# The second pair of gate and up tiles in products of 256 columns instead of 512

## The chip, the cores and the metric

The kernel runs on one core of a Trainium2 chip. The metric is the time of one execution in device microseconds (us). TensorE does the matrix products, VectorE (DVE) and ScalarE (ACT) the elementwise work, GpSimd (POOL) small work and some transfers, and SyncE (SP) issues most transfers. Products are written into PSUM, which has eight banks of 128 x 512 float32; everything else that the engines read lies in SBUF.

## The reference

One decoder layer on 512 tokens of 1024 features: a half-step SwiGLU network, a token mixer (sparse and dilated attention), and a second half-step SwiGLU network, each between two RMS norms.

```python
D_MODEL, SEQ, D_FF = 1024, 512, 2816

def swiglu(x, w_gate, w_up, w_down):
    return (jax.nn.silu(x @ w_gate) * (x @ w_up)) @ w_down

h = rms_norm(x, ffn1_pre)
x = x + 0.5 * rms_norm(swiglu(h, ffn1_w_gate, ffn1_w_up, ffn1_w_down), ffn1_post)
h = rms_norm(x, mix_pre)
x = x + rms_norm(token_mixer(h, ...), mix_post)
h = rms_norm(x, ffn2_pre)
x = x + 0.5 * rms_norm(swiglu(h, ffn2_w_gate, ffn2_w_up, ffn2_w_down), ffn2_post)
```

## The kernel before

"Part one" and "part two" are here the two SwiGLU networks; both run through `ffn`, part one with `opened` set (what `opening` has prepared), part two without. The token mixer lies between them.

**Products.** Every float32 operand is kept as a high and a low part (`split`, lines 139 to 141: ScalarE casts the high part at line 140, VectorE subtracts it from the source for the low part at line 141). `mm3` (lines 161 to 165) makes a product from three: high x high, high x low, low x high. Each of the three loads its own 128 x 128 weights and streams the activations `xhl` past them, up to 512 columns, one column a token.

**The hidden columns.** The 2816 hidden columns are 22 tiles of 128, taken as 11 pairs; index `p` is the pair, `f` the tile in it, `h` the half of the 1024 features (four blocks of 128), and `n` is gate or up. The first two pairs (`PLAIN = 2`) are computed directly; `mms` multiplies one half of one tile with all 512 tokens: four blocks, three products each, so 12 products of 512 columns. The other nine pairs use a scheme that multiplies sums of blocks (a fast matrix product with seven products in place of eight, named P1 to P7); `product` makes each from 24 products of 256 columns.

**Pair 0 and pair 1.** Pair 0 of part one is made in `opening`, which also makes the first half of pair 1's first tile; these are lines 1666 and 1696, 512 columns wide, and a full-precision product at line 1697 spreads the norm's row. In `ffn`, pair 1 of part one is then three calls' worth of weights, 72 products, and pair 1 of part two is four, 96. In part two pair 0 is made in 256 columns at a time, since its activations arrive token tile by token tile. `entered` splits one weight tile of 128 x 1024 into `whi` and `wlo` (three buffers each) and refills its raw buffer. `swiglu` multiplies and activates a finished pair of banks, `sums` makes sums of the results and stores them.

**The idle products.** Ahead of P1 of pair 2, `run` puts four products (`RESET`, lines 540 to 542) whose result is overwritten: 128 x 256, weights and activations both taken from the last weight tile of pair 1. They go into the bank that P1 opens.

**Order.** A scheduler orders each engine's instructions when the program is built, by its own estimate of times; what stands on an engine runs in that order. `PS_TAGS` gives the banks in turn (three S, two T, one V, two F).

Of the kernel before, what the change touches and what calls it, by code (L numbers as in the profile page):

```python
# [62 lines left out]
class Layer:  # L63
# [92 lines left out]
    def wsplit(self, src, shape):  # L156
        hi, lo = self.wpair(shape)
        self.split(hi, lo, src)
        return hi, lo

    def mm3(self, out, lhi, llo, rhi, rlo, start, stop, skip=False):
        mm = self.nc.tensor.matmul
# [175 lines left out]
    def ffn(self, gu, wd, td, post, finish, xsrc, aside=None, opened=None):  # L338
# [25 lines left out]
        def mms(w, h, n, b, lo=0, hi=S):  # L364
            c = slice(lo, hi)
            for j in range(4):
                k = 4 * h + j
                self.mm3(b[:, c], w[0][n][:, j], w[1][n][:, j], self.xh[k][:, c], self.xl[k][:, c], k == 0, k == KT - 1)

        def weight_sums(p):  # L370

            put = nc.gpsimd.dma_start
# [93 lines left out]
            return w  # L466

        for p in range(PLAIN):
            acts = []
            for f in range(2):  # L470
                key = 2 * p + f
                if p:
                    ws = [None if (key, 0) in banks and h == 0 else entered(p, h, f) for h in range(2)]
                    bs = [banks[key, n] if (key, n) in banks else self.bank() for n in range(2)]
                    for h in range(2):
                        for n in range(2):
                            if ws[h]:
                                mms(ws[h], h, n, bs[n])
                else:
                    bs = [banks[f, n] for n in range(2)]  # L480
                act = self.slot("W" if f else "ring")
                swiglu(act, bs[0], bs[1], slice(0, S))
                acts.append(act)
            sums(p, *acts)
            if p == 0 and not opened:
                tops = self.token_sums(t_tags)
            split_even(p)
# [43 lines left out]
        def run(p, name):  # L531
# [5 lines left out]
            if start:  # L537
                st[bank] = self.bank()
            with self.tc.issue_after(self.last_mm):
                if p == PLAIN and name == "P1":  # L540
                    for _ in range(RESET):
                        nc.tensor.matmul(st[bank][:, 0:256], self.last_w[:, 0], self.last_w[:, 2:4].rearrange("p k f -> p (k f)"), start=True, stop=True)
                product(w, top, st[bank], start)

        def finished(i, p, name):
# [1057 lines left out]
    def opening(self, gu, wd, td):  # L1603
# [37 lines left out]
        with self.tc.manual_schedule(engines={ET.Activation, ET.DVE, ET.PE}):  # L1641
# [51 lines left out]
            for n in range(2):  # L1693
                for k in range(4):
                    c = slice((4 * n + k) * P, (4 * n + k + 1) * P)
                    self.mm3(banks[4 + n], w[0][:, c], w[1][:, c], xh[k], xl[k], k == 0, False)
            nc.tensor.matmul(rowb, ones, diag, start=True, stop=True)
            row = self.slot("PT")
            nc.scalar.copy(row, rowb)
# [77 lines left out]
```

## Time and profile before

| | us |
|---|---|
| median of 3 runs | 1118.05 (1117.5 to 1119.21) |
| the profiled execution | 1118.12 |
| its span, first to last instruction | 1116.4 |

| engine | busy us | share of the span |
|---|---|---|
| TensorE products | 1095.6 | 98% |
| TensorE weight loads | 973.9 | 87% |
| VectorE | 883.4 | 79% |
| ScalarE | 642.4 | 58% |
| GpSimd | 187.7 | 17% |

Where things lie in the span: `opening` up to 34 us, pair 1 of part one from there to 51 us, the other nine pairs to 224 us, the down product behind them; part two has pair 0 from 783 us, pair 1 from 807 to 831 us and the nine pairs to 1003 us.

How to read the views: a row of the order of time gives the start, the duration, the engine, the line, the operation, the tile written and the tiles read, the shapes, and the count; in square brackets stands idle time of the engine before it and what ended it. A row of stretches gives, for each engine, its busy time in the stretch and in brackets how many instructions touch it, then the granted clock of TensorE, the busy share of the transfer engines and their GB/s. Products overlap, so their durations add up to more than the time between their starts.

### The profile page before, as it was taken

Reading aid. Unit: us, or ns where it says so; the run is one execution under the profiler, and the core shown is the slowest. Engines: PE = TensorE matmul, PEld = TensorE weight load, DVE = VectorE, ACT = ScalarE, POOL = GpSimd, SP = SyncE. Lnnn points to the kernel's source line nnn. Section 1 sums busy time; section 2 is a strip of 40 time slices with the busy share of each in tenths; the row PEclk is TensorE's granted clock in tenths of the full one; section 3 lists DMA queues with packets and bytes.
Section 4 is the critical chain, followed back from the end, with each engine's and each line's share of the span. In section 5 each row is a group of like instructions: output and inputs, shape, how many; then the busy total and the mean of one; then the engine's idle time right before and its main releaser. Section 6 shows DMA issues by size and latency. Waiting matters only on the chain.

```text
span 1116.4 us, 18585 instructions
## 1 busy us (share of the span) xinstructions
PE 1095.6 (98%) x6878; PEld 973.9 (87%) x6878; DVE 883.4 (79%) x1554; ACT 642.4 (58%) x1151; POOL 187.7 (17%) x264
## 2 busy tenths in 40 slices
PE   9999999999999999999999999999999999999997
PEld 7899999978889887777888898887989999998886
DVE  6989999988787889787554556876878999989575
ACT  7455555566565778675565625644435555557452
POOL 0444454310020055472000000000000000000001
PEclk9999999999999999999999999999999999999999
DMA  9999999999863499993224426383334444478862
GB/s 350 254 286 326 302 270 301 290 312 334 291 210 105 152 274 291 283 248 84 76 85 133 126 85 163 122 314 107 107 120 123 137 142 128 130 226 292 283 188 103
DMA packets 115595, 227.53 MB, mean 204 GB/s; under 512 B 21905, under 2 KB 51633, under 8 KB 115505
## 3 DMA queue, kind: packets, MB, share of 16 engines
q1 hardware_dynamic: 99136, 174.18, 47.8%
q0 software_dynamic: 16224, 51.91, 18.4%
q8 instruction: 54, 0.88, 0.3%
q14 instruction: 37, 0.30, 0.1%
q10 hardware_dynamic: 144, 0.26, 0.1%
HBM read 191.66 MB, written 57.72 MB: 223 GB/s over the span
## 4 chain that ended last, share of the span: by engine, by line
PE 76%; DVE 10%; ACT 4%; DMA 4%; issue 3%; POOL 1%; SPq 0%; POOLq 0%; DVEq 0%; ACTq 0%
PE pb_F L165 9%; PE pb_F L164 9%; PE pb_F L163 9%; PE pb_S L165 7%; PE pb_S L164 7%; PE pb_S L163 7%; PE pb_T L165 5%; PE pb_T L163 5%; PE pb_T L164 5%; PE pb_V L163 2%; PE pb_V L164 2%; PE pb_V L165 2%; DVE wlo L141 2%; DMA tdram<-in_d_dram 2%; PE pb_T L1666 1%
## 5 line engine op out<-in xcount | busy, mean ns | idle before, releaser
L141 DVE TENSOR_TENSOR wlo<-raw,whi 128x1024 fp32r<-128x1024 f32 (+1 forms) x211 | 248.5, 1183 | 125.3 <-ACT whi L140 122.6
L140 ACT CAST whi<-raw 128x1024 fp32r<-128x1024 f32 (+1 forms) x211 | 214.5, 1018 | 167.2 <-PE pb_F L164 41.9
L163 PE MATMUL pb_F<-xhl_t,whi 128*128 128x512 f32 (+1 forms) x440 | 155.1, 352 | 1.9 <-DVE Q_s L1409 1.0
L165 PE MATMUL pb_F<-xhl_t,wlo 128*128 128x512 f32 (+1 forms) x440 | 153.8, 350 | 1.3 <-DVE wlo L141 1.3
L164 PE MATMUL pb_F<-xhl_t,whi 128*128 128x512 f32 (+1 forms) x440 | 153.7, 349 | 0.0
L184 POOL TENSOR_TENSOR rs_t<-rs_t,mhalf_t 128x1 f32<-128x1 f32 x20 | 13.2, 659 | 558.2 <-DVE rs_t L180 558.2
L163 PEld LDWEIGHTS pb_F<-xhl_t,whi 128*128 128x128 f32 x440 | 82.8, 188 | 12.3 <-DVE Q_s L1409 1.2
L165 PEld LDWEIGHTS pb_F<-xhl_t,wlo 128*128 128x128 f32 x440 | 82.8, 188 | 11.8 <-DVE wlo L141 2.1
L164 PEld LDWEIGHTS pb_F<-xhl_t,whi 128*128 128x128 f32 x440 | 82.8, 188 | 9.6 <-issue 0.2
L163 PE MATMUL pb_S<-xhl_t,whi 128*128 128x256 f32 (+1 forms) x280 | 83.3, 297 | 0.0
L164 PE MATMUL pb_S<-xhl_t,whi 128*128 128x256 f32 (+1 forms) x280 | 83.1, 297 | 0.0
L165 PE MATMUL pb_S<-xhl_t,wlo 128*128 128x256 f32 (+1 forms) x280 | 82.8, 297 | 0.0
L1158 POOL TENSOR_SCALAR SP_s<-SP_s,st_t 128x384 f32<-128x384 f32 (+2 forms) x48 | 49.0, 1093 | 74.3 <-DMA raw<-in_w_in_dram 48.7
L163 PE MATMUL pb_T<-xhl_t,whi 128*128 128x256 f32 x200 | 55.4, 277 | 0.0
L164 PE MATMUL pb_T<-xhl_t,whi 128*128 128x256 f32 x200 | 55.4, 277 | 0.0
L165 PE MATMUL pb_T<-xhl_t,wlo 128*128 128x256 f32 x200 | 55.4, 277 | 0.0
L165 PEld LDWEIGHTS pb_S<-xhl_t,wlo 128*128 128x128 f32 x280 | 52.6, 188 | 2.2
L164 PEld LDWEIGHTS pb_S<-xhl_t,whi 128*128 128x128 f32 x280 | 52.6, 188 | 2.2
L163 PEld LDWEIGHTS pb_S<-xhl_t,whi 128*128 128x128 f32 x280 | 52.6, 188 | 2.2
L140 ACT CAST whi<-tmp_t 128x1024 fp32r<-128x1024 f32 x36 | 36.4, 1052 | 30.4 <-DVE tmp_t L512 23.5
L373 POOL DMA_DIRECT2D PT_s<-in_d_dram x44 | 39.1, 987 | 32.5 <-DMA PT_s<-in_d_dram 24.6
L141 DVE TENSOR_TENSOR PT_s<-pb_T,PT_s 128x512 fp32r<-128x512 f32 (+1 forms) x72 | 39.2, 558 | 6.8 <-ACT PT_s L140 6.1
(852 smaller groups left out, 3342.9 us busy)
## 6 DMA issues: line engine op xcount, KB each, us to landing
raw<-in_gu_dram SPq DMA_DIRECT2D x64, 512.0 KB, 4.6
raw<-tdram SPq DMA_DIRECT2D x40, 512.0 KB, 5.2
raw<-in_w_in_dram SPq DMA_DIRECT2D x18, 1024.0 KB, 5.4
PT_s<-in_d_dram POOLq DMA_DIRECT2D x66, 256.0 KB, 6.6
raw<-in_d_dram SPq DMA_DIRECT2D x30, 512.0 KB, 4.6
tdram<-in_d_dram POOLq DMA_DIRECT2D x18, 768.0 KB, 10.6
tdram<-PT_s POOLq DMA_DIRECT2D x44, 256.0 KB, 5.5
CP_s<-in_gu_dram SPq DMA_DIRECT2D x20, 512.0 KB, 3.9
```

The costliest lines, as they stand in the source:

```text
L140: self.last_cast = self.nc.scalar.copy(dsthi, src).ins
L141: self.last_sub = self.nc.vector.tensor_sub(dstlo, src, dsthi.bitcast(F32)).ins
L163: mm(out, lhi, rhi, start=start, stop=False, skip_group_check=skip)
L164: mm(out, lhi, rlo, start=False, stop=False, skip_group_check=skip)
L165: self.last_mm = mm(out, llo, rhi, start=False, stop=stop, skip_group_check=skip).ins
L184: nc.gpsimd.tensor_tensor(out=r, in0=v, in1=self.mhalf, op=OP.pow)
L373: add = lambda dst, src: put(dst, src, accum_op=OP.add)
L1158: self.last_pool = nc.gpsimd.tensor_scalar(pp, pp, st[:, 1, t:t + 1], None, op0=OP.mult).ins
L1666: nc.tensor.matmul(banks[b], l[:, c], r, start=k == 0 and i == 0, stop=k == KT - 1 and i == 2)
```

## The change

The products of pair 1 in `ffn` are made by a new function, `mms2`, which makes each product of 512 columns as two of 256; both write into the same bank, so only the first one of a bank starts it. The four idle products become a function, `reset`. In part one they stand ahead of pair 1's first product and no longer ahead of P1; in part two they stay where they were. To have a bank for them, part one takes the two banks of pair 1's second tile earlier.

```diff
+    def reset(self, b):
+        for _ in range(RESET):
+            self.nc.tensor.matmul(b[:, 0:256], self.last_w[:, 0], self.last_w[:, 2:4].rearrange("p k f -> p (k f)"), start=True, stop=True)
...
+        def mms2(w, h, n, b):
+            for j in range(4):
+                k = 4 * h + j
+                for m in range(2):
+                    c = slice(256 * m, 256 * m + 256)
+                    self.mm3(b[:, c], w[0][n][:, j], w[1][n][:, j], self.xh[k][:, c], self.xl[k][:, c], k == 0 and m == 0, k == KT - 1, True)
...
-            acts = []
+            acts, fresh = [], []
...
-                    bs = [banks[key, n] if (key, n) in banks else self.bank() for n in range(2)]
+                    bs = [banks[key, n] for n in range(2)] if (key, 0) in banks else fresh or [self.bank() for _ in range(2)]
                     for h in range(2):
                         for n in range(2):
                             if ws[h]:
-                                mms(ws[h], h, n, bs[n])
+                                if opened and f == 0 and n == 0:
+                                    fresh.extend(self.bank() for _ in range(2))
+                                    self.reset(fresh[0])
+                                mms2(ws[h], h, n, bs[n])
...
-                if p == PLAIN and name == "P1":
-                    for _ in range(RESET):
-                        nc.tensor.matmul(st[bank][:, 0:256], self.last_w[:, 0], self.last_w[:, 2:4].rearrange("p k f -> p (k f)"), start=True, stop=True)
+                if p == PLAIN and name == "P1" and not opened:
+                    self.reset(st[bank])
...
-                    self.mm3(banks[4 + n], w[0][:, c], w[1][:, c], xh[k], xl[k], k == 0, False)
+                    self.mm3(banks[4 + n], w[0][:, c], w[1][:, c], xh[k], xl[k], k == 0, False, True)
```

The rows that follow are the order of instructions as built; the kernel after has its lines 4 to 13 further down (163 is there the idle product, 167 to 169 are `mm3`, and 1710 is 1697).

TensorE at the end of part one's opening, before: the full-precision product, then the first products of pair 1.

```order
L165 MATMUL pb_S_139<-xhl_t_110,wlo_327 128x512
L1697 MATMUL pb_V_140<-W_s_363,cd_t_132 128x512 [waits DVE_49]
L163 MATMUL pb_F_138<-xhl_t_110,whi_454 128x512 [waits Activation_49]
L164 MATMUL pb_F_138<-xhl_t_110,whi_454 128x512
L165 MATMUL pb_F_138<-xhl_t_110,wlo_455 128x512
```

And the same place in the change:

```order
L169 MATMUL pb_S_139<-xhl_t_110,wlo_327 128x512
L1710 MATMUL pb_V_140<-W_s_363,cd_t_132 128x512 [waits DVE_49]
L163 MATMUL pb_S_459<-whi_454 128x256 [waits Activation_49]
L163 MATMUL pb_S_459<-whi_454 128x256 x3
L167 MATMUL pb_F_138<-xhl_t_110,whi_454 128x256
L168 MATMUL pb_F_138<-xhl_t_110,whi_454 128x256
L169 MATMUL pb_F_138<-xhl_t_110,wlo_455 128x256
```

The idle products now follow the full-precision one, read the high part of pair 1's first weight tile, and the products behind them are 256 wide.

TensorE in pair 1 of part two, before, at the point where the second weight tile is first used (its high part is `whi_8949`, its low part `wlo_8950`; 24 products of the pair stand ahead of these rows):

```order
L163 MATMUL pb_F_8954<-xhl_t_8433,whi_8949 128x512 [waits Activation_49]
L164 MATMUL pb_F_8954<-xhl_t_8433,whi_8949 128x512
L163 MATMUL pb_S_8955<-xhl_t_8433,whi_8949 128x512
L164 MATMUL pb_S_8955<-xhl_t_8433,whi_8949 128x512
L163 MATMUL pb_S_9017<-xhl_t_8433,whi_9007 128x512 [waits Activation_49]
L164 MATMUL pb_S_9017<-xhl_t_8433,whi_9007 128x512
L163 MATMUL pb_S_9018<-xhl_t_8433,whi_9007 128x512 [waits DVE_49]
L164 MATMUL pb_S_9018<-xhl_t_8433,whi_9007 128x512
L165 MATMUL pb_F_8954<-xhl_t_8433,wlo_8950 128x512 [waits DVE_49]
```

And in the change, where 48 products of the pair stand ahead:

```order
L167 MATMUL pb_F_9026<-xhl_t_8505,whi_9021 128x256 [waits Activation_49]
L168 MATMUL pb_F_9026<-xhl_t_8505,whi_9021 128x256
L167 MATMUL pb_S_9027<-xhl_t_8505,whi_9021 128x256
L168 MATMUL pb_S_9027<-xhl_t_8505,whi_9021 128x256
L167 MATMUL pb_S_9137<-xhl_t_8505,whi_9127 128x256 [waits Activation_49]
L168 MATMUL pb_S_9137<-xhl_t_8505,whi_9127 128x256
L167 MATMUL pb_S_9138<-xhl_t_8505,whi_9127 128x256 [waits DVE_49]
L168 MATMUL pb_S_9138<-xhl_t_8505,whi_9127 128x256
L169 MATMUL pb_F_9026<-xhl_t_8505,wlo_9022 128x256 [waits DVE_49]
```

In both programs the scheduler has lifted eight products that need only high parts over the one that waits for the low part; they were 512 wide and are 256 wide now.

VectorE in part one, around `sums` of pair 0 and the split of P1's weights (the row of `wlo`), before:

```order
L404 TENSOR_TENSOR W_s<-W_s,pb_S 128x512
L411 TENSOR_TENSOR of_s<-ring_s 128x256
L410 TENSOR_TENSOR of_s<-ring_s,W_s 128x256
L412 TENSOR_TENSOR ring_s<-of_s,ring_s 128x256
L413 TENSOR_TENSOR ring_s<-W_s,ring_s 128x256
L141 TENSOR_TENSOR wlo<-raw,whi 128x1024
L141 TENSOR_TENSOR Q_s<-ring_s,Q_s 128x512
L404 TENSOR_TENSOR ring_s<-ring_s,pb_S 128x512
L411 TENSOR_TENSOR of_s<-ring_s 128x256
```

And in the change (lines 413, 415 and 421 to 424 are 402, 404 and 410 to 413 of before):

```order
L415 TENSOR_TENSOR W_s<-W_s,pb_S 128x512
L422 TENSOR_TENSOR of_s<-ring_s 128x256
L421 TENSOR_TENSOR of_s<-ring_s,W_s 128x256
L413 TENSOR_TENSOR pb_F<-pb_F,PT_s 128x512
L423 TENSOR_TENSOR ring_s<-of_s,ring_s 128x256
L424 TENSOR_TENSOR ring_s<-W_s,ring_s 128x256
L141 TENSOR_TENSOR Q_s<-ring_s,Q_s 128x512
L415 TENSOR_TENSOR ring_s<-ring_s,pb_S 128x512
L422 TENSOR_TENSOR of_s<-ring_s 128x256
L141 TENSOR_TENSOR wlo<-raw,whi 128x1024
```

The split of P1's weights now stands behind the split of pair 0's result and two instructions of pair 1's. ScalarE moves its half of that split in the same way; on SP one store of `odram` goes behind one load of weights in part one, and one load of weights goes ahead of such a store in part two. GpSimd's order is the same.

## Prediction

> **What bounds the kernel now.** I read the page's chain of work first, then the stretches around the two places that the change touches, then the order of time on TensorE there.
>
> ```profile
> PE 76%; DVE 10%; ACT 4%; DMA 4%; issue 3%; POOL 1%; SPq 0%; POOLq 0%; DVEq 0%; ACTq 0%
> ```
> ```profile
> core 0: us, PE busy (x) PEld busy (x) DVE busy (x) ACT busy (x) POOL busy (x), PEclk, DMA share, GB/s
> 50.00:220.00 170.00, 169.88 (x1491) 169.41 (x1490) 162.83 (x225) 93.46 (x127) 77.67 (x103) 1.00 1.00 293
> 807.00:831.00 24.00, 23.27 (x103) 18.57 (x102) 17.89 (x22) 7.45 (x10) 0.00 (x0) 1.00 0.28 93
> 831.00:1003.00 172.00, 172.00 (x1513) 171.91 (x1512) 158.35 (x203) 96.84 (x136) 0.00 (x0) 1.00 0.49 148
> ```
>
> TensorE carries three quarters of the chain. In the long stretches behind the two pairs (50 to 220 and 831 to 1003) it is busy all the time at a granted clock of 1.00, so there the time is the number of products times the distance between their starts. The pair of part two (807 to 831) is the exception: 0.73 us idle. So I need two things: the distance from start to start by width, and what ends that idle time.
>
> Busy durations of products overlap and do not give the distance; first start, last start and count do.
>
> ```profile
> 35.00:51.00 16.00, 16.00 (x70) 1.00 0.94 253
> 53.00:203.00 150.00, 150.00 (x1326) 1.00 1.00 291
> 798.00:803.00 5.00, 5.00 (x45) 1.00 0.07 15
> 987.00:1003.00 16.00, 16.00 (x138) 1.00 0.85 282
> ```
> ```profile
> 33.73 1.02 PE L1697 MATMUL pb_V<-W_s,cd_t 128*128 128x512 f32 x2
> 34.19 0.80 PE L163 MATMUL pb_F<-xhl_t,whi 128*128 128x512 f32 x1
> 34.82 0.39 PE L164 MATMUL pb_F<-xhl_t,whi 128*128 128x512 f32 x1
> ...
> 51.15 0.39 PE L165 MATMUL pb_S<-xhl_t,wlo 128*128 128x512 f32 x1
> 51.39 0.63 PE L542 MATMUL pb_S<-whi 128*128 128x256 f32 x4
> 51.85 0.29 PE L163 MATMUL pb_S<-xhl_t,whi 128*128 128x256 f32 x1
> ...
> 52.55 0.28 PE L163 MATMUL pb_S<-xhl_t,whi 128*128 128x256 f32 x1
> ```
>
> From the product at 34.82 to the one at 51.15 are 70 steps (the first row's count): 16.33 / 70 = 233.3 ns for 512 columns. Of the 1,326 products that touch 53 to 203, two or three lie on its edges: 150 / 1,323.5 = 113.3 ns for 256 columns. The same width also runs slower: 45 products touch 798 to 803, so 5.00 / 42.5 = 117.7 ns, and 16.00 / 135.5 = 118 ns from 987 to 1003. And behind the four idle products the first six need 0.70 us (51.85 to 52.55), 117 ns each, before the rate settles. So the distance at one width has several steady values, and it is held for hundreds of products.
>
> Part two, TensorE and then VectorE:
>
> ```profile
> 807.26 0.28 PE L164 MATMUL pb_S<-xhl_t,SP_s 128*128 128x256 f32 x1
> 807.38 0.28 PE L165 MATMUL pb_S<-xhl_t,SP_s 128*128 128x256 f32 x1
> 807.50 0.40 PE L163 MATMUL pb_F<-xhl_t,whi 128*128 128x512 f32 x1
> ...
> 814.74 0.40 PE L164 MATMUL pb_S<-xhl_t,whi 128*128 128x512 f32 x1
> 815.87 0.50 PE L165 MATMUL pb_F<-xhl_t,wlo 128*128 128x512 f32 x1 [0.73 <-DVE wlo L141]
> 816.20 0.40 PE L163 MATMUL pb_F<-xhl_t,whi 128*128 128x512 f32 x1
> ...
> 830.90 0.64 PE L542 MATMUL pb_T<-whi 128*128 128x256 f32 x4
> 831.38 0.28 PE L163 MATMUL pb_T<-xhl_t,whi 128*128 128x256 f32 x1
> ```
> ```profile
> 812.86 0.68 DVE L141 TENSOR_TENSOR Q_s<-ring_s,Q_s 128x512 fp32r<-128x512 f32 x1
> 813.46 1.22 DVE L632 TENSOR_TENSOR tmp_t<-tmp_t,xhl_t 128x1024 f32<-128x1024 f32 x1
> 814.59 3.49 DVE L141 TENSOR_TENSOR wlo<-raw,whi 128x1024 fp32r<-128x1024 f32 x3
> ```
>
> The products of 256 ahead of the pair stand 120 ns apart (807.26, 807.38, 807.50). 32 products on, TensorE stands: the next one needs the second weight tile's low part, which VectorE makes as the first of the three at 814.59 (ready near 815.8). VectorE has no idle mark in these rows, and nothing that it does before them depends on the pair. So the wait's end, 815.87, is fixed by VectorE, and only what is left for TensorE behind it counts.
>
> **The change, part by part.** *Part one:* 72 products of 512 become 144 of 256, and the four idle ones move ahead of them, behind the full-precision product L1697. Before: from 34.19 to 51.39 the pair, to 51.85 the idle ones, to 52.55 six products at the slower rate: 18.36 us. After: the 34.19 row is the first idle product. The step from it to the next start is 0.63 us now, 0.40 more than one 512 step, which is what L1697 still holds; so the second idle product starts near 34.19 + 0.40 + 0.11 = 34.70, three more at the 115 ns of 51.39 to 51.85 (0.46 us for four) end near 35.05, six products settle in 0.70, and 138 at 113.3 take 15.64: 51.39. Then P1's first six at 113.3 take 0.68: 52.07 instead of 52.55. **Minus 0.48 us.** Of it 72 x (233.3 - 226.6) = 0.48 is the width; the idle products cost what they did.
>
> What must keep up: part one's VectorE order also shifts, the low part of P1's weights going behind three small instructions.
>
> ```profile
> 41.28 1.22 DVE L141 TENSOR_TENSOR wlo<-raw,whi 128x1024 fp32r<-128x1024 f32 x1 [0.29 <-ACT whi L140]
> 42.42 0.68 DVE L141 TENSOR_TENSOR Q_s<-ring_s,Q_s 128x512 fp32r<-128x512 f32 x1
> 43.02 0.68 DVE L404 TENSOR_TENSOR ring_s<-ring_s,pb_S 128x512 f32<-128x512 f32 x1
> 43.73 0.42 DVE L411 TENSOR_TENSOR of_s<-ring_s 128x256 f32<-128x256 f32 x1
> ```
>
> It ends at 42.50 now and some 2 us later then (0.68 + 0.68 + 0.42 go ahead, and one of them waits for the first pair half); it is wanted at 51.4. Nothing: the cover is the second half of the pair. On SP a store and a load of a tile change places; all later weights come from loads issued long before, so I take nothing.
>
> *Part two:* 96 products become 192, without idle products ahead. The scheduler lifts eight rows over the wait in both programs, but now they are halves: 48 + 8 = 56 halves stand ahead of the wait, against 24 + 8 = 32 whole ones. Left behind it are 136 halves, 68 wholes' worth instead of 64. The rate of the 56 doesn't matter, since the wait covers it (56 x 0.118 = 6.6 us ends near 814.1, before 815.8). The 64 whole products behind it take 15.03 us today, 815.87 to 830.90. The 136 halves take a restart step of 0.22 (next fence) and 135 steps of 113.3 ns: 15.52. **Plus 0.49 us**: eight more halves cost 0.91, and the width gives back 64 x 6.7 ns = 0.43. If the rate ahead of the idle products is already 113.3, P1 saves 0.03 of settling. The trace does not show which rate follows this wait. Bounds from restarts of TensorE on the same activations:
>
> ```profile
> 790.59 0.38 PE L163 MATMUL pb_F<-xhl_t,whi 128*128 128x256 f32 x1 [0.21 <-DVE xhl_t L241]
> 790.81 0.28 PE L164 MATMUL pb_F<-xhl_t,whi 128*128 128x256 f32 x1
> 790.92 0.28 PE L165 MATMUL pb_F<-xhl_t,wlo 128*128 128x256 f32 x1
> ```
> ```profile
> 986.71 0.39 PE L165 MATMUL pb_T<-SP_s,wlo 128*128 128x256 f32 x1
> 986.94 0.28 PE L163 MATMUL pb_T<-SP_s,whi 128*128 128x256 f32 x1
> 987.05 0.28 PE L164 MATMUL pb_T<-SP_s,whi 128*128 128x256 f32 x1
> 987.17 0.28 PE L165 MATMUL pb_T<-SP_s,wlo 128*128 128x256 f32 x1
> ```
>
> The first, a wait in which TensorE ran empty, comes back at 113 at once; the second, a hitch without idle time, at 118. The wait here is of the first kind and longer, so I take 113.3; the other end is 0.22 + 135 x 0.120 = 16.4 us, +1.4.
>
> *Sum:* -0.48 + 0.49 - 0.03 = **-0.02 us** on the profiled execution's 1118.12 us (span 1116.4, so 1.7 around it; median of the runs 1118.05). Part one's gain may also be lost at the next DMA on the chain,
>
> ```profile
> 235.94 8.03 DMA SP_s<-sxdram
> ```
>
> a load of 8 us whose end VectorE and then TensorE wait for: between 0 and 0.48 of it survives. I keep the sum: **1118.1**. Its bounds are 1117.5 (the shift also spares the slow stretch from 987 to 1003, 138 x 4.4 ns = 0.6) and 1119.5 (120 ns behind the wait, +0.9 against the sum, and nothing left of part one's 0.48).
>
> The Trainium skill (TensorE: Matmul & The Clock Gate, Back-to-back issue gap) gives the warm distance as the columns by 2.4 GHz plus a fixed 2.5 ns, so 109 and 216 ns, and two halves 2.5 ns dearer than a whole. The rows above (2 x 113.3 against 233.3) say the opposite at the steady rate. By the Trainium skill part one would lose 72 x 2.5 ns, an estimate of 0.2 us, in place of its gain.
>
> **Rivals.** *Halves that cost more than wholes, in the pairs alone.* At 117.7 to 120 ns two halves take 235 to 240 against 233.3. For: 807.26 to 807.50 runs so directly ahead. Against: 53 to 203. Price: part one 144 x 0.1177 to 0.120 - 72 x 0.2333 = +0.15 to +0.5, part two +1.1 to +1.4: 1119.3 to 1120.0. The fixed cost of the Trainium skill's page has this sign too.
>
> *The slow rate is carried into the rest of a part (slower).* The four idle products are followed by the 113 rate at both of their places, each time directly behind products of 512. After the change neither place is so: in part one they stand behind L1697, in part two behind products of 256 at whatever rate. If the rate behind them is 117.7 or 120, the whole stretch of some 1,500 products goes with it (1,491 and 1,513 in the table of stretches), as 987 to 1003 shows one carried to its end: 1,500 x 4.4 to 6.7 ns = +6.6 to +10 us, near 1124.7 for one part at 117.7. It decides at the first settled product behind the idle ones: over 114 ns, it is this case. Against it: tiles change dozens of times from 53 to 203 without leaving 113.
>
> *More gained than summed (faster).* If VectorE's tile came before TensorE asks for it, part two would take 192 x 0.1133 = 21.8 us instead of 23.4 (807.50 to 830.90): -1.6; with part one -2.1, and with the 0.6 of 987 to 1003 near 1115.4. Against: no instruction ahead of that tile leaves VectorE's list.
>
> **How the numbers follow.** My forecast 0.58, halves dearer in the pairs alone 0.12, slow rate carried on 0.22, more gained 0.05, the rest 0.03 for stalls I don't see. 0.2% is 2.2 us, about what a measurement can tell from no change here. Same: the first two, 0.70. Slower: 0.24. Faster: 0.06. The forecast's own range is 1117.5 to 1119.5. To leave out no more than 2 in 10 the range must reach into the carried slow rate, to one part at 117.7: 1125; below, to 1116.5, part of the third rival. Left out are two slow parts or 120 ns, and the deepest gains.
>
> **What would show it.** Right: 113 ns from about 35.8 on, P1 of part one starting near 51.4; TensorE's wait in part two longer (some 1.7 us) and still ending at 815.4 or so, with the idle products near 830.9 again on the shifted clock; 113 ns behind them. Wrong: 118 or 120 ns behind either group of idle products; a wait in part two that ends earlier than 814.5; a new wait in P1 or P2.

## The result and the profile after

| | kernel before | changed kernel |
|---|---|---|
| median of the runs | 1118.63 us (1116.6 to 1119.9, 6 runs) | 1126.7 us (1123.62 to 1132.3, 6 runs) |
| ratio | | 1.0084, 95% interval 1.0068 to 1.0100 |
| profiled execution, its own time | 1118.12 us | 1132.3 us |
| span | 1116.4 us | 1130.5 us |

The change makes the kernel slower, by 8.1 us from median to median and by 0.84% in the ratio; the forecast was no change, 1118.1 us. The changed kernel's six runs lie in two groups, four from 1123.6 to 1127.0 and two at 1131.1 and 1132.3. The profiled execution is the slowest of them, so what follows accounts for its 14.2 us (1132.3 less 1118.12) and not for the median's 8.1. The four lower runs would fit one of the two losses found below in place of both; none of them was profiled. Of all the runs below, one counts as slow and is left out of its kernel's ratio: 1132.95 us, of the changed kernel without any idle products.

The chain of work of the changed kernel, shares of the span by engine (TensorE's was 76% before):

```profile
PE 77%; DVE 9%; DMA 5%; ACT 4%; issue 3%; POOL 2%; SPq 0%; POOLq 0%; DVEq 0%; ACTq 0%
```

TensorE's table of stretches, for the kernel before and then for the changed one. The columns are the stretch, its length, TensorE's busy time with the number of products that touch the stretch, the granted clock, the DMA share and GB/s.

```profile
36.00:50.00 14.00, 14.00 (x62) 1.00 0.94 258
53.00:203.00 150.00, 150.00 (x1326) 1.00 1.00 291
816.00:830.00 14.00, 14.00 (x61) 1.00 0.36 112
842.00:982.00 140.00, 140.00 (x1237) 1.00 0.45 134
```
```profile
36.00:50.00 14.00, 14.00 (x121) 1.00 0.88 236
53.00:203.00 150.00, 150.00 (x1275) 1.00 0.99 285
824.00:838.00 14.00, 14.00 (x126) 1.00 0.36 114
842.00:982.00 140.00, 140.00 (x1191) 1.00 0.44 131
```

TensorE is full and at clock 1.00 in all eight rows. What differs is how many products fit. With the 2.5 that lie on a stretch's edges taken off, the two long stretches hold one product per 113.3 to 113.4 ns before (150 / 1,323.5 and 140 / 1,234.5) and one per 117.8 to 117.9 ns after (150 / 1,272.5 and 140 / 1,188.5). The third pair of rows shows the opposite: part two's pair in halves runs at 113 ns (14 / 123.5). So the halves themselves are fast there, and the products of the nine pairs behind them, which the change didn't touch, are slow.

Where each rate begins is seen in TensorE's order of time of the changed kernel (start, busy time, both in us; line 163 is the idle product, lines 167 to 169 are the three products of `mm3`):

```profile
33.84 1.02 PE L1710 MATMUL pb_V<-W_s,cd_t 128*128 128x512 f32 x2
34.29 1.04 PE L163 MATMUL pb_S<-whi 128*128 128x256 f32 x4
35.17 0.28 PE L167 MATMUL pb_F<-xhl_t,whi 128*128 128x256 f32 x1
...
52.13 0.28 PE L167 MATMUL pb_S<-xhl_t,whi 128*128 128x256 f32 x1
...
230.21 0.39 PE L167 MATMUL pb_F<-whi,Q_s 128*128 128x512 f32 x1
```
```profile
821.58 0.28 PE L168 MATMUL pb_S<-xhl_t,whi 128*128 128x256 f32 x1
823.47 0.38 PE L169 MATMUL pb_F<-xhl_t,wlo 128*128 128x256 f32 x1 [1.61 <-DVE wlo L141]
...
838.89 0.28 PE L169 MATMUL pb_S<-xhl_t,wlo 128*128 128x256 f32 x1
839.00 0.63 PE L163 MATMUL pb_T<-whi 128*128 128x256 f32 x4
839.47 0.28 PE L167 MATMUL pb_T<-xhl_t,whi 128*128 128x256 f32 x1
...
1017.55 0.39 PE L167 MATMUL pb_F<-whi,Q_s 128*128 128x512 f32 x1
```

The 144 halves of part one's pair take 52.13 - 35.17 = 16.96 us, 117.8 ns each, and the rate goes on to the end of the nine pairs at 230.21. In part two the rate is 113 ns from the wait's end to the idle products at 839.00, and 117.8 behind them. The wait of TensorE is 1.61 us long, and VectorE sets its end, the first of three low parts (VectorE's order of time):

```profile
822.20 3.49 DVE L141 TENSOR_TENSOR wlo<-raw,whi 128x1024 fp32r<-128x1024 f32 x3
```

In the kernel before, the first product of the stage behind each part stands at

```profile
223.63 0.39 PE L163 MATMUL pb_F<-whi,Q_s 128*128 128x512 f32 x1
...
1003.54 0.40 PE L163 MATMUL pb_F<-whi,Q_s 128*128 128x512 f32 x1
```

so the 14.2 us divide as follows, by these rows and those of the prediction:

| stretch | before, us | after, us | difference |
|---|---|---|---|
| start to the first row behind part one's full-precision product | 34.19 | 34.29 | +0.1 |
| part one, from there to the end of the nine pairs | 34.19 to 223.63: 189.44 | 34.29 to 230.21: 195.92 | +6.5 |
| from there to the wait's end in part two | 223.63 to 815.87: 592.24 | 230.21 to 823.47: 593.26 | +1.0 |
| part two's pair behind the wait | 815.87 to 830.90: 15.03 | 823.47 to 839.00: 15.53 | +0.5 |
| part two, idle products to the end of the nine pairs | 830.90 to 1003.54: 172.64 | 839.00 to 1017.55: 178.55 | +5.9 |
| the rest, with what lies around the span | | | +0.2 |

12.4 of the 14.2 us lie in the two stretches from the idle products on. The 1.0 us between the parts has no row that ties it to the change.

### The profile page after: what moved, and what is told of

Same layout as the page of the kernel before. It is cut to its first block, busy times and chain, and to the rows that moved or that the text cites. A ratio compares the mean times of both kernels' runs of the same rounds, so it can differ in the third digit from the quotient of the medians.

```text
span 1130.5 us, 18923 instructions
## 1 busy us (share of the span) xinstructions
PE 1107.7 (98%) x7046; PEld 994.3 (88%) x7046; DVE 883.5 (78%) x1554; ACT 643.4 (57%) x1151; POOL 190.7 (17%) x264
## 4 chain that ended last, share of the span: by engine, by line
PE 77%; DVE 9%; DMA 5%; ACT 4%; issue 3%; POOL 2%; SPq 0%; POOLq 0%; DVEq 0%; ACTq 0%
PE pb_F L169 9%; PE pb_F L168 9%; PE pb_F L167 9%; PE pb_S L168 7%; PE pb_S L169 7%; PE pb_S L167 7%; PE pb_T L169 5%; PE pb_T L168 5%; PE pb_T L167 5%; PE pb_V L167 2%; PE pb_V L168 2%; PE pb_V L169 2%; DMA tdram<-in_d_dram 2%; DVE wlo L141 2%; PE pb_T L1679 1%
## 5 line engine op out<-in xcount | busy, mean ns | idle before, releaser
L167 PE MATMUL pb_F<-xhl_t,whi 128*128 128x512 f32 (+1 forms) x452 | 157.3, 348 | 2.4 <-DVE Q_s L1422 1.3
L169 PE MATMUL pb_F<-xhl_t,wlo 128*128 128x512 f32 (+1 forms) x452 | 156.4, 346 | 2.1 <-DVE wlo L141 2.1
L168 PE MATMUL pb_F<-xhl_t,whi 128*128 128x512 f32 (+1 forms) x452 | 156.3, 346 | 0.0
L167 PEld LDWEIGHTS pb_F<-xhl_t,whi 128*128 128x128 f32 x452 | 85.3, 189 | 12.1 <-DVE Q_s L1422 1.5
L169 PEld LDWEIGHTS pb_F<-xhl_t,wlo 128*128 128x128 f32 x452 | 85.3, 189 | 12.0 <-DVE wlo L141 2.8
L168 PEld LDWEIGHTS pb_F<-xhl_t,whi 128*128 128x128 f32 x452 | 85.0, 188 | 8.9
L167 PE MATMUL pb_S<-xhl_t,whi 128*128 128x256 f32 (+1 forms) x324 | 91.4, 282 | 0.0
L168 PE MATMUL pb_S<-xhl_t,whi 128*128 128x256 f32 (+1 forms) x324 | 91.2, 282 | 0.0
L169 PE MATMUL pb_S<-xhl_t,wlo 128*128 128x256 f32 (+1 forms) x324 | 91.0, 282 | 0.0
L167 PEld LDWEIGHTS pb_S<-xhl_t,whi 128*128 128x128 f32 x324 | 61.6, 190 | 0.2
L169 PEld LDWEIGHTS pb_S<-xhl_t,wlo 128*128 128x128 f32 x324 | 61.1, 189 | 0.2
L168 PEld LDWEIGHTS pb_S<-xhl_t,whi 128*128 128x128 f32 x324 | 60.9, 188 | 0.2
L167 PE MATMUL pb_S<-SP_s,whi 128*128 128x256 f32 x160 | 45.0, 281 | 0.0
L169 PE MATMUL pb_S<-SP_s,wlo 128*128 128x256 f32 x160 | 45.0, 281 | 0.0
```

What stands on the lines that cost most here:

```text
L167: mm(out, lhi, rhi, start=start, stop=False, skip_group_check=skip)
L168: mm(out, lhi, rlo, start=False, stop=False, skip_group_check=skip)
L169: self.last_mm = mm(out, llo, rhi, start=False, stop=stop, skip_group_check=skip).ins
```

## The experiments

After the result, the theory was that the rate of a long stretch of 256 column products is set where the stretch is entered and then held, and that the four idle products had set it to 113 ns before and set it to 117.7 now. The rivals were the edits beside it: halves that cost more, the full-precision product ahead (L1710 in the changed kernel), and VectorE's new order in part one.

All readings use one view: the number of products of TensorE in 53 to 203 us (part one) and 842 to 982 us (part two). About 1,326 and 1,238 mean 113.3 ns, about 1,276 and 1,191 mean 117.8 ns. The kernel before, run beside them, took 1116.96, 1117.28, 1116.95 and 1117.81 us; each of these goes with four rows of the table, in its order. Each set of four ran on another chip.

| kernel | rate in part one, part two (profiled execution) | median, us (lowest to highest) | ratio to before (95% interval) |
|---|---|---|---|
| changed, no idle products in part two | 118, 118 | 1129.16 (1128.67 to 1131.22) | 1.0114 (1.0094 to 1.0134) |
| changed, part one's idle products back ahead of P1 | 118, 118 | 1124.46 (1117.74 to 1131.53) | 1.0072 (1.0042 to 1.0103) |
| before, no idle products | 118, 118 | 1125.44 (1122.68 to 1128.14) | 1.0077 (1.0046 to 1.0107) |
| before, part one's idle products ahead of its pair of 512 | 118, 113 | 1118.11 (1115.71 to 1121.83) | 1.0013 (0.9997 to 1.0029) |
| halves in part one without idle products there | 113, 113 | 1122.48 (1114.9 to 1126.81) | 1.0035 (1.0018 to 1.0053) |
| changed, no idle products at all | 113, 113 | 1125.19 (1114.89 to 1132.95) | 1.0055 (1.0026 to 1.0085) |
| halves in part two alone | 113, 118 | 1124.71 (1123.71 to 1127.94) | 1.0069 (1.0054 to 1.0084) |
| changed, four idle products of 512 ahead of the four in part two | 118, 113 | 1124.17 (1122.96 to 1124.84) | 1.0058 (1.0045 to 1.0071) |
| the same in both parts | 113, 113 | 1120.56 (1117.66 to 1126.62) | 1.0039 (1.0020 to 1.0059) |
| one of 512 ahead in both parts | 118, 113 | 1125.97 (1121.47 to 1127.88) | 1.0070 (1.0047 to 1.0093) |
| changed, eight idle products | 113, 113 | 1119.08 (1116.39 to 1121.31) | 1.0013 (1.0002 to 1.0024) |
| changed, one idle product | 113, 113 | 1122.73 (1116.31 to 1126.89) | 1.0041 (1.0017 to 1.0064) |
| changed, two idle products | 118, 118 | 1129.63 (1117.04 to 1131.26) | 1.0080 (1.0047 to 1.0113) |
| changed, three idle products | 113, 113 | 1118.7 (1116.13 to 1123.32) | 1.0013 (1.0000 to 1.0026) |
| changed, six idle products | 113, 113 | 1119.44 (1116.97 to 1124.3) | 1.0016 (0.9999 to 1.0033) |
| before, eight idle products | 113, 113 | 1118.01 (1116.68 to 1119.1) | 1.0006 (0.9996 to 1.0015) |

A run's time doesn't always fit the rate that the one profiled execution of its kernel shows: several kernels with a wide spread have runs in groups some 6 us apart, which is about the price of one slow part. The rates below are those of the profiled executions, one for each kernel; what the other runs of a kernel did is inferred from their times alone.

### Are the idle products the culprit?

First, the changed kernel without part two's idle products:

```diff
-                if p == PLAIN and name == "P1" and not opened:
-                    self.reset(st[bank])
```

> The changed kernel without the four idle products in part two. Theory A (the idle products themselves throw a stretch that already runs at 113 ns out of that rate): behind the pair's 113 ns the nine pairs of part two go on at 113 ns, part two's stretch takes 171 to 172 us instead of 178, and the kernel is about 7 us faster than the changed one. Theory B (a pair made of halves leads into the slow rate, idle products or none): 118 ns behind the pair, no gain but the 0.5 us of the idle products. Part one stays as in the change under both.

TensorE's table of stretches, and its order of time where the rate breaks:

```profile
53.00:203.00 150.00, 150.00 (x1276) 1.00 0.98 284
842.00:982.00 140.00, 140.00 (x1191) 1.00 0.43 130
```
```profile
840.97 0.28 PE L169 MATMUL pb_T<-xhl_t,wlo 128*128 128x256 f32 x1
841.09 0.34 PE L167 MATMUL pb_T<-SP_s,whi 128*128 128x256 f32 x1
841.26 0.28 PE L168 MATMUL pb_T<-SP_s,whi 128*128 128x256 f32 x1
841.38 0.28 PE L169 MATMUL pb_T<-SP_s,wlo 128*128 128x256 f32 x1
```

P1 and the products up to 841.09 ran at 113 ns here, and nothing threw them at P1's entry. So the idle products did that in the changed kernel. At 841.09 one product is some 0.06 us late (0.17 to the next start in place of 0.11), and from there the rate is 117.8 to the end. Here a small hitch did what the idle products did, and the time is no better. It need not: in the changed kernel without any idle products, told below, the same product is as late, 0.05 us, and the rate behind it stays at 113:

```profile
833.75 0.28 PE L169 MATMUL pb_T<-xhl_t,wlo 128*128 128x256 f32 x1
833.86 0.33 PE L167 MATMUL pb_T<-SP_s,whi 128*128 128x256 f32 x1
834.03 0.28 PE L168 MATMUL pb_T<-SP_s,whi 128*128 128x256 f32 x1
834.14 0.28 PE L169 MATMUL pb_T<-SP_s,wlo 128*128 128x256 f32 x1
```

Second, the changed kernel with part one's idle products back ahead of P1, behind the halves:

```diff
-                                if opened and f == 0 and n == 0:
-                                    fresh.extend(self.bank() for _ in range(2))
-                                    self.reset(fresh[0])
...
-                if p == PLAIN and name == "P1" and not opened:
+                if p == PLAIN and name == "P1":
```

> The changed kernel with part one's idle products back ahead of P1, so that both parts have the pair in halves and then the idle products. Theory A: whatever rate part one's pair has, the idle products behind halves give 118 ns in both parts, as slow as the changed kernel. A rival (it is the full-precision product just ahead that spoils the idle products in part one): part one's nine pairs run at 113 ns, some 7 us faster than the changed kernel, part two as slow as there.

```profile
50.87 0.28 PE L167 MATMUL pb_S<-xhl_t,whi 128*128 128x256 f32 x1
50.98 0.28 PE L168 MATMUL pb_S<-xhl_t,whi 128*128 128x256 f32 x1
51.09 0.28 PE L169 MATMUL pb_S<-xhl_t,wlo 128*128 128x256 f32 x1
51.21 0.63 PE L163 MATMUL pb_S<-whi 128*128 128x256 f32 x4
51.67 0.28 PE L167 MATMUL pb_S<-xhl_t,whi 128*128 128x256 f32 x1
51.79 0.28 PE L168 MATMUL pb_S<-xhl_t,whi 128*128 128x256 f32 x1
```

Steps of 0.11 us ahead of the four idle products, 0.12 behind them. The halves of part one run at 113 ns directly behind the full-precision product, so that product alone doesn't lead to 118. The ten runs fall in three groups, 1117.7 to 1118.1, 1123.1 to 1124.5 and 1129.9 to 1131.5. The steps of some 6 us fit no, one and two slow parts; only one execution, of the slowest group, was profiled. If that reading is right, four idle products behind halves don't lead to 118 in every run.

Third, the kernel before without its idle products:

```diff
-                if p == PLAIN and name == "P1":
-                    for _ in range(RESET):
-                        nc.tensor.matmul(st[bank][:, 0:256], ...)
```

> The kernel before without its idle products in either part. If the idle products are what brings the nine pairs to 113 ns behind products of 512: 118 to 120 ns in both parts, 7 to 10 us slower each, 1125 to 1138 us. If products of 512 alone lead into 113 ns, as at 782.84 in the trace of before, where 256 follows 512 with no idle product between: 113 ns in both parts, and 0.9 us faster than before, 1117.5 us.

Fourth, the kernel before with part one's idle products ahead of its pair, which stays 512 wide:

```diff
+                                if opened and f == 0 and n == 0:
+                                    fresh.extend(self.bank() for _ in range(2))
+                                    self.reset(fresh[0])
...
-                if p == PLAIN and name == "P1":
-                    for _ in range(RESET):
...
+                if p == PLAIN and name == "P1" and not opened:
...
```

> The kernel before with part one's idle products moved ahead of its pair, the pair left in products of 512. Theory A: the idle products no longer matter to part one, whose nine pairs follow products of 512 directly; 113 ns if 512 alone leads into it, 118 to 120 ns if idle products are needed there (7 to 10 us slower). Part two is as before, 113 ns. A rival, that the scheduler's other order on VectorE costs the time: a slower part one at 113 ns, with waits of TensorE.

The stretches of these two, in the same order:

```profile
53.00:203.00 150.00, 150.00 (x1276) 1.00 0.98 283
842.00:982.00 140.00, 140.00 (x1191) 1.00 0.44 132
```
```profile
53.00:203.00 150.00, 150.00 (x1276) 1.00 0.99 282
842.00:982.00 140.00, 140.00 (x1238) 1.00 0.45 133
```

Behind products of 512 it is the other way round in the profiled executions: without idle products between, the stretch runs at 117.8 in both parts, and the kernel before loses 8.5 us (1125.44 against 1116.96). Its four runs are two at 1122.7 to 1122.9 and two at 1128.0 to 1128.1; the profiled one is of the upper two, and the lower two would fit one slow part. The second kernel has VectorE's new order in part one, with products of 512; it is slow there in the profiled execution, where nothing stands between the 512 and P1, as the first one is. That execution, 1121.73, is one of four from 1121.2 to 1121.8; the other six, 1115.7 to 1118.2, lie within the range of the kernel before beside it (1114.80 to 1119.46), and so does the median. So VectorE's order costs nothing that shows in them, and a direct entry from 512 doesn't seem to be slow every time. The kernel before has one that is not: at 782.84 products of 256 follow 512 without idle ones, and after steps of 118, 116, 118, 122 and 119 ns they run at 113.

### One part at a time, and none of the idle products

Halves in part one with no idle products there, part two as before (against the changed kernel):

```diff
-                                if opened and f == 0 and n == 0:
-                                    fresh.extend(self.bank() for _ in range(2))
-                                    self.reset(fresh[0])
-                                mms2(ws[h], h, n, bs[n])
+                                (mms2 if opened else mms)(ws[h], h, n, bs[n])
```

> Part one's pair in halves with no idle products anywhere in part one; part two as before the change. Theory (the rate of a stretch is set where it is entered; halves enter at 113 ns by themselves, and the idle products are needed only behind products of 512): 113 ns from about 35 us to the end of P1 and P2 of part one, and against the kernel before -0.48 us for the width, -0.46 for the idle products and their slot: 1116.0 us where the kernel before takes 1117.0. Rival (without the idle products any short hitch throws the stretch, as it did in part two at 841.09): 113 ns at first, then 117.7 from the hitch on, +4 to +6 us, 1121 to 1123. Second rival (the rate at entry differs from execution to execution): times in two clusters some 6 us apart, near 1116 and 1122.5.

The changed kernel without any idle products:

```diff
-                                if opened and f == 0 and n == 0:
-                                    fresh.extend(self.bank() for _ in range(2))
-                                    self.reset(fresh[0])
...
-                if p == PLAIN and name == "P1" and not opened:
-                    self.reset(st[bank])
```

> The changed kernel without any idle products. Theory: part one at 113 ns from about 35 us on, since nothing stands ahead of the halves that throws them (so L1697 isn't what throws it), part two as in the changed kernel without part two's idle products, 113 ns to P6 and 117.7 from there: before -0.9 +5.9, about 1122. Rival (the place behind L1697 leads to 117.7 with or without idle products): part one slow too, near 1129, as the changed kernel without part two's idle products alone gave.

The stretches of the two, in this order:

```profile
53.00:203.00 150.00, 150.00 (x1326) 1.00 1.01 296
842.00:982.00 140.00, 140.00 (x1238) 1.00 0.46 137
```
```profile
53.00:203.00 150.00, 150.00 (x1326) 1.00 1.01 295
842.00:982.00 140.00, 140.00 (x1238) 1.00 0.46 137
```

Both profiled executions run at 113 in both parts and take 1114.90 and 1114.89 us; the kernel before has 1114.80 as its lowest. But of the twelve runs of the first seven lie from 1122.0 to 1126.8, and of the second seven lie above 1122, four of these at 1129 and more. Without idle products the 113 can be had and isn't kept from run to run: the second rival of the first expectation. The part of the theory that halves enter at 113 "by themselves" holds for the executions in the profile only.

Halves in part two alone, part one as before:

```diff
-                                if opened and f == 0 and n == 0:
-                                    fresh.extend(self.bank() for _ in range(2))
-                                    self.reset(fresh[0])
-                                mms2(ws[h], h, n, bs[n])
+                                (mms if opened else mms2)(ws[h], h, n, bs[n])
...
-                if p == PLAIN and name == "P1" and not opened:
+                if p == PLAIN and name == "P1":
```

> Part one as before, part two's pair in halves with the idle products behind them as in the changed kernel. Theory: part one 113 ns throughout, part two 113 ns for 129 halves behind the wait, then 117.7 for some 1,511 products behind the idle ones: +6.6 us, 1123.5. Rival (a whole kernel's rates differ only by chance, and halves have nothing to do with it): times like the kernel before, near 1117, or clusters 6 us apart of which the lower holds half.

```profile
53.00:203.00 150.00, 150.00 (x1326) 1.00 1.00 293
842.00:982.00 140.00, 140.00 (x1191) 1.00 0.43 128
```

As the theory had it: 7.4 us over the kernel before (1124.71 against 1117.28), in all four runs, and only part two is slow.

### What ahead of the idle products decides?

The changed kernel with four idle products of 512 columns directly ahead of the four in part two:

```diff
-    def reset(self, b):
+    def reset(self, b, wide=0):
+        for _ in range(wide):
+            self.nc.tensor.matmul(b, self.last_w[:, 0], self.last_w[:, 0:4].rearrange("p k f -> p (k f)"), start=True, stop=True)
...
-                    self.reset(st[bank])
+                    self.reset(st[bank], 4)
```

> The changed kernel, with four idle products of 512 columns put directly ahead of the four idle ones in part two. Theory (what stands directly ahead of the idle products decides: behind 512 they lead to 113, behind 256 at 113 they throw it to 117.7): part two at 113 ns again behind them, part one slow as in the changed kernel: 1117.0 + 6.6 in part one + 0.9 for the four wide products + 0.0 = 1124.5. Rival (the halves of the pair, or the tiles' order, make part two slow, whatever stands right ahead of the idle ones): 117.7 there still, near 1131.

```profile
53.00:203.00 150.00, 150.00 (x1276) 1.00 0.99 285
842.00:982.00 140.00, 140.00 (x1238) 1.00 0.44 131
```

1124.17 against the 1124.5 expected. Part two is at 113 again although its pair is in halves, so neither the halves nor the tiles' order in part two cost the 6 us. What stands just ahead of P1 does. The four wide ones also make it eight idle products in place of four, so this run can't tell their width from their number.

With four wide ones in both parts, and with one in both:

```diff
-                                    self.reset(fresh[0])
+                                    self.reset(fresh[0], 4)
```

> The changed kernel, with four idle products of 512 columns directly ahead of the four idle ones in both parts. Theory (directly behind products of 512 the four idle ones lead to 113 ns, whatever the pair's width): 113 ns from about 36 us and from the idle products of part two, so 1117.0 - 0.5 + 2 x 0.93 = 1118.4, with the runs in one cluster. Rival (the halves cost the 6 to 7 us of each part in another way, or part one's place behind L1710 does): part one still 117.7 ns, near 1125.

> As the kernel with four wide idle products in both parts, with one wide product in place of four. If one product of 512 directly ahead is enough: 113 ns in both parts, 1117.0 - 0.5 + 2 x 0.23 = 1117.0. If it takes several (the distance has to settle at 233 ns first): 117.7 ns behind them in one part or both, 1123.5 or 1130.

The stretches of the one with a single wide product:

```profile
53.00:203.00 150.00, 150.00 (x1276) 1.00 0.99 285
842.00:982.00 140.00, 140.00 (x1237) 1.00 0.45 137
```

With four in both parts the profiled execution runs at 113 throughout, but the ten runs don't lie in one group as expected: three of them are at 1125.5 to 1126.6. A single wide product is enough in part two and not in part one, where it stands behind the full-precision product and not behind 256 column products. In part two the pair ran at 118 in this execution, from the wait's end on; the other twelve kernels with this pair in halves have the same TensorE instructions from the wait to the pair's end and ran at 113 there. So one place came out at either rate with the same neighbours.

### How many idle products?

Up to here the theory read: behind 512 the idle products lead to 113, behind halves they throw it to 117.7. Only their number is changed now, in both parts.

```diff
-RESET = 4
+RESET = 8
```

> The changed kernel with eight idle products in place of four, in both parts. Theory (idle products behind 256 columns end at 117.7 ns): still 117.7 in both parts, 1126.7 + 2 x 0.46 = 1127.6, and never below 1123. Rival (it is a matter of their number: four more bring the distance back to 113): 113 ns in one part or both, 1121 or 1118.

And with one (`RESET = 1`):

> The changed kernel with one idle product in place of four, in both parts. Theory (any product that breaks the pattern of three, two of them on the same weights, throws 113 to 117.7): 117.7 in part two behind it, and in part one 113 or 117.7 as without idle products: 1123 to 1130. Rival (one repeated product is too little to throw it): part two at 113 behind the idle product, at 113 until a hitch such as the one at 841.09 without idle products; 1117 to 1123.

The stretches with eight:

```profile
53.00:203.00 150.00, 150.00 (x1326) 1.00 1.00 294
842.00:982.00 140.00, 140.00 (x1238) 1.00 0.45 134
```

The theory in that form fell. Eight idle products behind halves bring 113 in both parts, and with one the profiled execution is at 113 too, though six of its ten runs lie from 1122.3 to 1126.9. The time with eight, 1119.08, is 2.1 us over the kernel before and not the 10.7 of the expectation. So what stands ahead isn't all that decides; two, three and six were tried (`RESET` alone is changed, as above), and eight behind the 512 of the kernel before:

> The changed kernel with two idle products in place of four, in both parts. If their number decides together with what stands ahead (the distance passes through a sequence of steps behind the first idle product, and the stretch locks where the sequence stands when the real products come): part two either 113 or 117.7, the same in all executions whose pair ran at 113, so times in at most two clusters 6 us apart, 1116.6 or 1123. If any four or fewer but one fail because they end in the same slow run: 117.7 in both parts, 1130.

> The changed kernel with three idle products in place of four, in both parts. By the number's theory either rate, and it need not be that of two or four; by the width's theory (halves ahead throw it) 117.7 in part two, 1123 to 1130.

> The changed kernel with six idle products in place of four, in both parts. If eight recovered because enough idle products let the distance settle, six lie between: 113 in part one at least, 1117 to 1124. If only the exact number counts, either rate; if the halves ahead throw it, 117.7 in both, 1130.

> The kernel before with eight idle products in place of four, behind its products of 512. Theory (behind 512 idle products lead to 113 whatever their number): 1117.0 + 2 x 0.46 = 1117.9, all runs within 3 us. Rival (number and neighbour act together, and four was right for 512 only): 117.7 in one part or both, 1124 or 1130.

The stretches with two idle products, and with three:

```profile
53.00:203.00 150.00, 150.00 (x1276) 1.00 0.98 285
842.00:982.00 140.00, 140.00 (x1192) 1.00 0.43 130
```
```profile
53.00:203.00 150.00, 150.00 (x1326) 1.00 1.01 296
842.00:982.00 140.00, 140.00 (x1237) 1.00 0.44 136
```

One idle product more, 0.12 us of work in each part, and the median is 10.9 us lower (1118.7 against 1129.63). Most runs bear this out: seven of nine with two lie above 1125, nine of ten with three at or below 1121. Two and four idle products behind halves are followed by 117.8 in part two; one, three, six and eight by 113. Behind 512, four and eight are followed by 113, and the eight lie within 1116.7 to 1119.1, as expected. In part two a pair in halves ends at 113 in all the rows below, so the entry can be followed from start to start (ns, worked out from the starts in the traces; in brackets the steps between idle products):

| idle products, part two | steps from the first idle product on | then |
|---|---|---|
| 1 | 119, 118, 125, 118, 113 | 113 |
| 2 | (119) 113, 117, 117, 118, 118 | 118 |
| 3 | (119, 113) 116, 122, 116, 114, 113 | 113 |
| 4, halves in part two alone | (119, 112, 117) 118, 119, 119, 117, 118 | 118 |
| 6 | (119, 113, 117, 118, 119) 121, 113, 124, 115, 115, 113 | 113 |
| 8 | (119, 113, 116, 119, 119, 121, 116) 118, 121, 121, 116, 114 | 113 |
| 4, behind 512 (kernel before) | (116, 118, 120) 120, 114, 123, 116, 114, 113 | 113 |

Behind halves, with two idle products or more, the steps begin alike, 119, 112 or 113, 116 or 117; the number seems to decide where along this sequence the real products come in. Four behind halves gave nearly the same steps in three kernels (the changed one and the one with the idle products back ahead of P1 are the other two); the other numbers have one execution each. In this table one or two longer steps of 121 to 125 ns near that point go with 113, and their absence with 118. It isn't a rule: with two idle products in part one, steps of 127, 121 and 122 came and the stretch settled at 118 nonetheless. Why a given entry ends at one rate or the other is left open.

## Why the prediction was wrong

**The step that failed.** In part one the sum let "three more at the 115 ns", then six products settle, "and 138 at 113.3", and it took P1 to follow at 113.3; in part two it took 113 behind the idle products as well. Both took over from the kernel before what follows four idle products, without a row for their new neighbours. The runs show that it isn't a property of the idle products: four behind 512 gave 113 in both parts of the kernel before, four behind halves gave 118 in part two alone (+7.4 us), and two, three and six behind halves gave 118, 113 and 113.

**The rival that came true** is the slow rate carried into the rest of a part, to which 0.22 was given. Its place (the first settled product behind the idle ones), its price (+6.6 us a part at 117.7 ns; measured +6.5 and +5.9) and its reason (the place is no longer directly behind 512) stood in the text; the four wide idle products fit the reason, the eight show that it isn't the whole of it. What spoke against it, that tiles change dozens of times from 53 to 203 without leaving 113, was true and beside the point: it says that a held rate survives changes of tile, not which rate an entry leads to. The prediction's own rows had a restart at 113 (790.59), one at 118 (986.71) and six steps of 117 ns behind the idle products; these were no ground for 0.22 against 0.58. And the range stopped at one slow part, though both places lose the same neighbour; the median lies 1.7 us above it.

**Part two's pair** was right. Wait longer, some 1.7 us expected, 1.61 measured; its end set by VectorE; 113 ns behind it; 15.52 us expected from the wait's end to the idle products, 15.53 measured. That 113 follows this wait was still a choice, as the prediction says: it did in twelve of the thirteen kernels with this pair in halves, and 118 in the other.

**Part one's pair** was wrong by the same step. Expected: P1 starts at 51.39, 0.46 earlier than before; measured: 52.13, 0.28 later, 144 x 4.4 ns = 0.6 of it by the rate. That 113 was possible shows in the kernel with the idle products back ahead of P1, whose idle products start at 51.21.

**VectorE's and SP's order** cost nothing that shows: P1 comes in without a wait at 52.13, and in the kernel before with VectorE's order the median stays within 0.3%.

**The fixed cost.** The Trainium skill (TensorE: Matmul & The Clock Gate, Back-to-back issue gap) has a fixed 2.5 ns a product, by which two halves are dearer than a whole; it gives this for the isolated gap of single products and says that in a stream with a weight load for each product both set the spacing. The products here are such a stream. At 117.7 ns they are, by 2.1 ns (2 x 117.7 against 233.3), at 113.3 cheaper by 6.7; which of the two held went with the entry here, and no single fixed cost fits both.

**Halves dearer in the pairs alone, and more gained:** neither. The first was true of part one's pair, but most of the 6.5 us lay behind it.

No kernel here beats the kernel before. The lowest single times of the others, 1114.89 and 1114.90, belong to kernels whose medians are 1125.19 and 1122.48, and 1114.80 came from the kernel before itself; the best that the width could give by the prediction's terms, 0.5 us in part one, is less than a measurement can tell.

## What to carry to other kernels

Where one kind of instruction shows several steady rates in a trace, an edit is priced first by the long stretches whose entry it touches and only then by its own instructions: here 168 more products moved 0.5 us and the rate of some 1,500 behind them 6 us a part. Where filler stands at such an entry, as the idle products do here, the rate went with its neighbours and its number, so when either changes the number is tried again, and the rate behind it is read from the count of products in a fixed stretch. A wide spread of a kernel's times, in groups one such price apart, can be a sign that its rate isn't settled by the program, and one profile then shows only one of the cases.

## What the runs showed of the hardware that was not expected

- 256 column products at a granted clock of 1.00 ran at 113.3 or at 117.8 ns a product for 1,300 to 1,650 products on end, TensorE full in both cases.
- A product some 0.06 us late (841.09, the changed kernel without part two's idle products) was followed by 118 ns in place of 113 for the remaining 1,460 or so of the stretch; one 0.05 us late at the same place (833.86, the changed kernel without any idle products) was not.
- The rate behind idle products went with their number in the profiled executions: 113, 118, 113, 118, 113, 113 ns for 1, 2, 3, 4, 6 and 8 of them behind halves in part two.
- The same TensorE instructions behind the same wait of 1.6 us ran at 113 ns in twelve kernels and at 118 in one.
- The same program on the same chip gave times in groups: 1117.7 to 1118.1, 1123.1 to 1124.5 and 1129.9 to 1131.5 for one kernel.
